# Where the low parts of some weights are made, and how far ahead branch B's operand is fetched, in a hybrid encoder layer

## The chip, the cores and the metric

The kernel runs on one core of a Trainium2 chip. The metric is device time in microseconds (us) for one execution, and the figure compared is the median of several runs. The engines are called by their names: TensorE (PE in the profile, its weight loads PEld) multiplies matrices, VectorE (DVE) and ScalarE (ACT) work elementwise, GpSimd (POOL) here only issues transfers, and SyncE (SP) issues nearly all other transfers. Every engine works through its own list of instructions in order. Sixteen DMA engines carry the transfers.

## The reference

One layer of an encoder with D = 1024, applied with the same weights to a prompt of 512 rows and a sample of 1024 rows, all in float32:

```
h = rms_norm(x, g_pre) * (1 + scale) + shift
p = h @ w_in                                   # 1024 x 8192
a_val, a_glu, a_z, u, v, b_z, g_a, g_b = split(p)
# branch A: convolution over time, 31 taps, per channel
hA = a_val * sigmoid(a_glu)
hA = silu(layer_norm(conv(hA) + conv_b)) * silu(a_z)
y_a = hA @ conv_proj
# branch B: gating over chunks of 128 rows
v  = layer_norm(gelu(v))
hB = gelu(u) * (w_s mixed over the rows of each chunk of v, + b_s) * silu(b_z)
y_b = hB @ sgu_proj
m  = sigmoid(g_a) * y_a + sigmoid(g_b) * y_b
out = x + gate * rms_norm(m @ w_out, g_post)
```

`shift`, `scale` and `gate` come from `silu(c) @ w_ada + b_ada`.

## The kernel before, in words

**Precision.** Each float32 operand X is split into a rounded high part Xh and a remainder Xl = X - Xh, and a product W X is three matmuls: Wh Xh, Wh Xl and Wl Xh. So every block of weights needs a high part `hi` and a low part `lo`, each 128x1024.

**A unit of weights.** One block of 512 KB is a `Unit`. `unit_load` has SyncE load it as `raw` (L222) four steps before its use; only four `raw` tiles exist, and four `hi` and four `lo`. `unit_act` runs about two and a half steps before the use: ScalarE casts `hi` from `raw` (L246). The low part is then made in one of two ways. With `by_dma` true, ScalarE writes -raw into `lo`, which rounds it to -hi (L249), and GpSimd issues a transfer that adds `raw` to it in place (L239, `lo<-raw` in the profile). With `by_dma` false, VectorE subtracts `hi` from `raw` (L258, `unit_dve`), and neither ScalarE's second pass nor the transfer is there.

**The steps.** TensorE's work is a list of steps, of 24 matmuls each where it multiplies by a block of weights (128x512 outputs, eight blocks of the contraction, three matmuls each):

| steps | work |
|---|---|
| 0 to 15 | prompt: convolution's value and gate columns |
| 16 to 23 | prompt: v (`steps_v`) |
| 24 to 79 | prompt: u, b_z, gates, a_z, the two projections (`col_step`) |
| 80 to 87 | prompt: w_out (`steps_o`) |
| 88 to 95, 96 to 103 | sample: v of half a, v of half b (`steps_v`) |
| 104 to 299 | sample: 28 pairs of column blocks, seven products each in place of eight (Strassen's way) |
| 300 to 315 | sample: branch B's projection of half a, then of half b (`post_B`) |
| 316 to 323, 324 to 331 | half a: branch A's projection (`post_A`), w_out |
| 332 to 339, 340 to 347 | half b: branch A's projection, w_out |

**What sets the order.** Python code writes the instructions out step by step: for each step it first emits the elementwise work that is due, then the matmuls, and then the loads that are due. Work that belongs to no step is a generator in the list `bg`; `fill` takes from it as long as a model clock of VectorE says that there is time. Small matmuls asked for by a generator are slipped into the middle of a step. `force` runs a generator to its end where a step needs its outcome. The model clock has constants written into the code, and no run goes back into it. So a line that is added for VectorE also moves where the generators' instructions stand on all engines.

**Around the sample's v.** While steps 88 to 103 run, a generator makes the operands of the pairs: sums and differences of halves of the sample (L928 to L936), with spills to and fetches from DRAM (`wk<-d`, L145). At the end of each half of v, VectorE takes the mean and variance (L544, L556), eight small matmul groups mix the rows of each chunk, and VectorE brings their outcomes out of PSUM (`mix_out`, L572). There are 8 PSUM banks in all.

**Around the end of the pairs.** The pairs spill hB, branch B's operand, to DRAM as eight blocks for each half. `hB_gen` fetches them again (L145), casts their high parts on ScalarE (L1266) and subtracts the low parts on VectorE (L1271). It runs for half a from step s_end - 6 = 294 and for half b from step 300, and fetches two blocks ahead. The convolution of the sample ends at about that place: its last outcome is stored to DRAM from `c` (L521, `d<-c`), and then `late_ln` fetches eight blocks of it (L145, `c<-d`) for its layer norm, which begins with small matmuls (L330, L331) on operands that ScalarE casts (L319). A little later the same pieces prepare branch A's operand (`hA`), whose low parts are written at L1231 and which half b needs from step 332.

Names in the profile: the matmuls of a column step are L448 to L450, of a step in `steps_v` or `steps_o` L471 to L473, and of the pairs L482 to L484; L1013 and L1125 are ScalarE's handling of the pairs' outcomes. Tiles: `wk` are 128x512 work tiles (11 buffers), `A` operand halves, `b` PSUM banks, `d` DRAM scratch.

Of the kernel before, what the change touches and what calls it, by code (L numbers as in the profile page):

```python
# [40 lines left out]
LAG = 1.0  # L41
PLAIN = 5.25
PROD = PLAIN / 2
LEAD_LOAD = 4 * PLAIN
LEAD_SPLIT = 2.4 * PLAIN

# [33 lines left out]
def layer_kernel(ctx: ExitStack, tc, x_p, x_s, xt_p, xt_a, xt_b, par, w_blk, w_v, cproj, sproj, w_out, w_ada, w_gate, wsT, bs,  # L80
# [121 lines left out]
    steps = []  # L202
# [167 lines left out]
    def start_bg(t, name, gen, first=False):  # L370
        setattr(t, name, gen)
        bg.insert(0, gen) if first else bg.append(gen)
# [118 lines left out]
        return st  # L491

    def col_step(t, src, act, a1=None, d1=None, d2=None, a2=None, pre=None, box=None, need=None, by_dma=True):
        u = Unit(src, len(steps), by_dma)

        def mm():
            b = bank()
            mm_cols(b, u, act())
            box[0] = b

        st = add_step(Step(mm, a1, d1, a2, d2, pre, need=need), u)

        def quarter(b, wh, wl, q):
            box[0] = b
            mm_quarter(b, wh, wl, act(), q)
        st.quarter = quarter
        return st
# [15 lines left out]
    def steps_v(t, need=None):  # L523

        for h in range(2):
            banks = []
            for kc in range(4):
                u = Unit(w_v[h, kc], len(steps))

                def mm(u=u, kc=kc, banks=banks):  # L530
                    if kc == 0:
                        banks[:] = [bank() for _ in range(4)]
                    mm_rows(banks, u, t.operand(), kc)

                def a1(h=h, banks=banks):
                    if h == 0:
                        t.v = t.v_home()
                        t.bn = smp.tile([P, 4, 12], F32, tag="bn", name="bn", bufs=1)
                    for i in range(4):
                        S.activation(t.v[:, i, h * T:(h + 1) * T], banks[i], AF.Gelu_apprx_tanh)  # L540

                def d1(h=h):
                    for i in range(4):
                        dv(0.65, lambda: V.bn_stats(out=t.bn[:, i, h * 6:h * 6 + 6], in_=t.v[:, i, h * T:(h + 1) * T]))  # L544

                def d2(h=h):
                    if h == 0:
                        return
                    mv = smp.tile([P, 4, 2], F32, tag="mv", name="mv")
                    for i in range(4):  # L550
                        dv(0.15, lambda: V.bn_aggr(out=mv[:, i, :], in_=t.bn[:, i, :].rearrange("p (c s) -> p c s", s=6)))
                    var = smp.tile([P, 4], F32, tag="ss", name="var")
                    dv(0.1, lambda: V.tensor_copy(var, mv[:, :, 1]))
                    r = rstd_small(var, 4, LN_EPS)
                    for i in range(4):
                        dv(0.65, lambda: V.tensor_scalar(t.v[:, i, :], t.v[:, i, :], mv[:, i, 0:1], r[:, i:i + 1],  # L556
                                                         op0=ALU.subtract, op1=ALU.mult))
                    if t.after_v:
                        t.after_v()
                last = kc == 3  # L560
                add_step(Step(mm, a1 if last else None, d1 if last else None, None, d2 if last else None,
                              act=2.2 if last else 0.0, need=need if h == 0 and kc == 0 else None), u)
# [20 lines left out]
    def steps_o(t, final, on_end=None):  # L583

        for h in range(2):
            banks = []
            for kc in range(4):
                u = Unit(w_out[h, kc], len(steps))

                def mm(u=u, h=h, kc=kc, banks=banks):  # L590
                    if kc == 0:
# [222 lines left out]
    sa, sb = Tile(), Tile()  # L814
# [177 lines left out]
    def pair(src1, src2, finish):  # L992
# [9 lines left out]
        def prod(name, wt, i, opn, first, last, a1=None, d1=None, a2=None, need=None, act=0.6):  # L1002
            def mm():
                if first:
                    st[name] = bank()
                mm_prod(st[name], half(w[wt][0], i), half(w[wt][1], i), A[opn], first, last)
            s_ = add_step(Step(mm, a1, d1, a2, dur=PROD, need=need, act=act))
            return s_
# [241 lines left out]
    def hB_gen(t):  # L1250
        xs = {}

        def fetch(j):
            if j < NK:
                x = wk()
                xs[j] = (x, load(x, outs["hB", t.half, j]))
        fetch(0)
        fetch(1)
        t.hB = new_act()
        kept = {}  # L1260
        for j in range(NK + 1):
            fetch(j + 2)
            if j < NK:
                x, tt = xs.pop(j)
                yield from until(tt)
                kept[j] = (x, ac(0.53, lambda: S.copy(t.hB.hi(j), x)))  # L1266
                yield "op"
            if j > 0:
                x, t1 = kept.pop(j - 1)
                yield from until(t1)  # L1270
                dv(0.62, lambda: V.tensor_sub(t.hB.lo(j - 1), x, t.hB.hi(j - 1).bitcast(F32)))  # L1271
                yield "op"
        t.hB_done = True
# [73 lines left out]
    def also(s, fn):  # L1347
        old = steps[s].extra

        def both():  # L1350
            if old:
                old()
            fn()
        steps[s].extra = both
# [17 lines left out]
        for j in range(0, NK, 2):  # L1372
            pair(w_blk[b0 + j], w_blk[b0 + j + 1], fin(j))
    s_end = len(steps)
    also(s_end - 6, lambda: start_bg(sa, "hBg", hB_gen(sa), first=True))
    post_B(sa)
    also(s_end, lambda: start_bg(sb, "hBg", hB_gen(sb), first=True))
    post_B(sb)
# [217 lines left out]
    for q in range(4):  # L1596
        for j in range(NH):
            u = q * NH + j
# [211 lines left out]
```

## Time and profile before

| | |
|---|---|
| runs | 1494.92, 1484.97 and 1494.02 us; median 1494.02 us |
| profiled execution | 1490.75 us, of which its span 1489.0 us |
| mean clock granted to TensorE | 0.986 of full speed |
| busy in the span | PE 1440.8 us (97%), PEld 1172.1 (79%), DVE 1089.2 (73%), ACT 776.4 (52%), POOL 216.9 (15%) |
| DMA | queue of SyncE 44.2% of 16 engines' span, queue of GpSimd 39.6% |

The busy time of an engine is the sum of its instructions' durations. In rows of windows the columns are the stretch, its length, then for each engine the busy time and, in brackets, the number of instructions, then the granted clock, the share of the DMA engines and what they moved. In rows of a timeline they are the start, the duration, the engine, the line, the operation and its tiles, the count, and in square brackets the idle time before the instruction with what ended it.

### The profile page before, as it was taken

To read this page: it belongs to the slowest core of one execution; us is meant where nothing else is said; L and a number is where in the kernel's file an instruction comes from. 1 tells how busy PE (TensorE), PEld (TensorE's weight loads), DVE (VectorE), ACT (ScalarE), POOL (GpSimd) and SP (SyncE) were. 2 spreads that over 40 slices of the span, in tenths; PEclk is the share of its full clock that TensorE was granted. 3 is DMA by queue.
4 is the path that set the end of the run, shared out by engine and by line. 5 is a ranking of instruction groups with operands and counts; after the bars stand their busy time and mean duration, and the time that the engine had idled before them with its cause. 6 is when DMAs were issued, how large, how long until landed. Compare 5 with 4: busy or idle time off the path is not lost.

```text
span 1489.0 us, 17873 instructions
## 1 busy us (share of the span) xinstructions
PE 1440.8 (97%) x6332; PEld 1172.1 (79%) x6332; DVE 1089.2 (73%) x1560; ACT 776.4 (52%) x1100; POOL 216.9 (15%) x256
## 2 busy tenths in 40 slices
PE   8999999999999998899999999999999969999997
PEld 4688888888888777788888888877878848888886
DVE  6769999985257344557999899889999847584424
ACT  4533545553685445454555565554556646556443
POOL 0001111111111111111111111111111101111110
PEclk9999999999999999999999999999999969999999
DMA  9268876998999999977666879987877799999994
GB/s 341 80 207 216 213 212 170 212 254 229 252 268 217 299 279 269 294 167 204 151 155 166 208 185 268 258 216 203 243 203 182 200 304 285 315 263 295 249 289 127
DMA packets 125225, 340.57 MB, mean 229 GB/s; under 512 B 13904, under 2 KB 17616, under 8 KB 124368
## 3 DMA queue, kind: packets, MB, share of 16 engines
q1 hardware_dynamic: 88992, 229.85, 44.2%
q0 software_dynamic: 36144, 109.59, 39.6%
q8 instruction: 49, 0.80, 0.2%
q14 instruction: 40, 0.33, 0.1%
HBM read 182.10 MB, written 47.71 MB: 154 GB/s over the span
## 4 chain that ended last, share of the span: by engine, by line
PE 68%; DMA 18%; DVE 7%; ACT 3%; issue 3%; SPq 2%; DVEq 0%; ACTq 0%; POOLq 0%
PE b L450 9%; PE b L449 9%; PE b L448 9%; PE b L482 9%; PE b L483 9%; PE b L484 9%; DMA raw<-in_w_blk_dram 4%; DMA raw<-in_w_v_dram 3%; DMA wk<-d 3%; PE b L471 3%; PE b L472 3%; PE b L473 3%; DMA c<-d 2%; DVE c L402 2%; DMA lo<-raw 1%
## 5 line engine op out<-in xcount | busy, mean ns | idle before, releaser
L448 PE MATMUL b<-A,hi 128*128 128x512 f32 x776 | 306.1, 394 | 10.7 <-ACT A L1266 10.7
L482 PE MATMUL b<-A,hi 128*128 128x512 f32 x784 | 306.3, 391 | 6.3 <-ACT wk L1013 6.3
L483 PE MATMUL b<-A,hi 128*128 128x512 f32 x784 | 305.2, 389 | 0.0
L484 PE MATMUL b<-A,lo 128*128 128x512 f32 x784 | 305.1, 389 | 0.0
L449 PE MATMUL b<-A,hi 128*128 128x512 f32 x776 | 305.1, 393 | 0.0
L450 PE MATMUL b<-A,lo 128*128 128x512 f32 x776 | 304.3, 392 | 0.3 <-DMA lo<-raw 0.2
L402 DVE SCALAR_TENSOR_TENSOR c<-c,prm 128x1024 f32<-128x1024 f32 x240 | 297.6, 1281 | 0.6
L246 ACT CAST hi<-raw 128x1024 fp32r<-128x1024 f32 x145 | 151.9, 1048 | 257.7 <-DMA raw<-in_w_v_dram 72.6
L239 POOL DMA_DIRECT2D lo<-raw x167 | 144.3, 864 | 797.0 <-ACT lo L249 695.3
L448 PEld LDWEIGHTS b<-A,hi 128*128 128x128 f32 x776 | 146.9, 189 | 43.8 <-ACT A L1266 13.3
L482 PEld LDWEIGHTS b<-A,hi 128*128 128x128 f32 x784 | 147.2, 188 | 39.4 <-ACT wk L1013 8.9
L449 PEld LDWEIGHTS b<-A,hi 128*128 128x128 f32 x776 | 146.8, 189 | 32.0 <-DVE A L1271 1.8
L450 PEld LDWEIGHTS b<-A,lo 128*128 128x128 f32 x776 | 147.0, 189 | 31.6 <-DMA lo<-raw 1.1
L484 PEld LDWEIGHTS b<-A,lo 128*128 128x128 f32 x784 | 147.2, 188 | 30.6
L483 PEld LDWEIGHTS b<-A,hi 128*128 128x128 f32 x784 | 147.2, 188 | 30.0
L402 DVE SCALAR_TENSOR_TENSOR S<-c,prm,S 128x512 f32<-128x512 f32 x240 | 162.5, 749 | 0.4
L472 PE MATMUL b<-lo,A 128*128 128x512 f32 x384 | 152.0, 396 | 9.1 <-DMA lo<-raw 9.1
L471 PE MATMUL b<-hi,A 128*128 128x512 f32 x384 | 152.3, 397 | 3.9 <-DVE wk L572 3.9
L473 PE MATMUL b<-hi,A 128*128 128x512 f32 x384 | 151.3, 394 | 0.0
L249 ACT ACTIVATE lo<-raw 128x1024 fp32r<-128x1024 f32 x139 | 146.7, 1056 | 0.0
L239 POOL DMA_DIRECT2D lo<-T x84 | 72.4, 862 | 448.0 <-ACT lo L1067 360.1
L1013 ACT COPY wk<-b 128x512 f32<-128x512 f32 x112 | 65.1, 586 | 119.8 <-PE b L484 116.1
(206 smaller groups left out, 1590.2 us busy)
## 6 DMA issues: line engine op xcount, KB each, us to landing
lo<-raw POOLq DMA_DIRECT2D x139, 512.0 KB, 6.9
raw<-in_w_blk_dram SPq DMA_DIRECT2D x105, 512.0 KB, 5.5
d<-wk SPq DMA_DIRECT2D x142, 256.0 KB, 3.9
wk<-d SPq DMA_DIRECT2D x116, 256.0 KB, 7.4
lo<-T POOLq DMA_DIRECT2D x28, 512.0 KB, 5.5
lo<-T POOLq DMA_DIRECT2D x56, 256.0 KB, 4.8
raw<-in_w_v_dram SPq DMA_DIRECT2D x24, 512.0 KB, 6.9
raw<-in_sproj_dram SPq DMA_DIRECT2D x24, 512.0 KB, 6.9
```

The costliest lines, as they stand in the source:

```text
L239: GP.dma_start(lo.bitcast(F32), src, accum_op=ALU.add)
L246: S.copy(u.hi, u.raw)
L402: lambda: V.scalar_tensor_tensor(acc, in0=win, scalar=wt, in1=acc, op0=ALU.mult, op1=ALU.add))
L448: PE.matmul(dst, lhsT=wh3[:, k, :], rhs=hi, start=(k == 0), stop=False)
L449: PE.matmul(dst, lhsT=wh3[:, k, :], rhs=lo, start=False, stop=False)
L450: PE.matmul(dst, lhsT=wl3[:, k, :], rhs=hi, start=False, stop=(k == NK - 1))
L471: PE.matmul(banks[i], lhsT=hi, rhs=wh3[:, kk, :], start=(k == 0), stop=False)
L472: PE.matmul(banks[i], lhsT=hi, rhs=wl3[:, kk, :], start=False, stop=False)
L473: PE.matmul(banks[i], lhsT=lo, rhs=wh3[:, kk, :], start=False, stop=(k == NK - 1))
L482: PE.matmul(dst, lhsT=wh3[:, k, :], rhs=hi, start=st, stop=False, skip_group_check=True)
L483: PE.matmul(dst, lhsT=wh3[:, k, :], rhs=lo, start=False, stop=False, skip_group_check=True)
L484: PE.matmul(dst, lhsT=wl3[:, k, :], rhs=hi, start=False, stop=sp, skip_group_check=True)
```

## The change

Three things are changed. First, in `steps_v` the units of odd steps get `by_dma` false, so that VectorE makes their low parts: 12 units, steps 17, 19, 21 and 23 of the prompt and 89 to 103 of the sample. Second, a constant `CONV_END = 88` makes the units of column steps and of w_out steps from step 88 on do the same at odd steps: 24 units in steps 300 to 347. Steps 24 to 87 stay with the transfer. Third, `hB_gen` fetches four blocks ahead in place of two, and for half a it is started at step 291 in place of 294; the operand's tile is still taken only from step 294 on (`hB_ok`).

```diff
+CONV_END = 88
 ...
     def col_step(t, src, act, a1=None, d1=None, d2=None, a2=None, pre=None, box=None, need=None, by_dma=True):
-        u = Unit(src, len(steps), by_dma)
+        u = Unit(src, len(steps), by_dma and (len(steps) < CONV_END or len(steps) % 2 == 0))
 ...
     def steps_v(t, need=None):
-                u = Unit(w_v[h, kc], len(steps))
+                u = Unit(w_v[h, kc], len(steps), len(steps) % 2 == 0)
 ...
     def steps_o(t, final, on_end=None):
-                u = Unit(w_out[h, kc], len(steps))
+                u = Unit(w_out[h, kc], len(steps), len(steps) < CONV_END or len(steps) % 2 == 0)
 ...
     def hB_gen(t):
-        fetch(0)
-        fetch(1)
+        for j in range(4):
+            fetch(j)
+        while not t.hB_ok():
+            yield "wait"
         t.hB = new_act()
         kept = {}
         for j in range(NK + 1):
-            fetch(j + 2)
+            fetch(j + 4)
 ...
-    also(s_end - 6, lambda: start_bg(sa, "hBg", hB_gen(sa), first=True))
+    also(s_end - 9, lambda: start_bg(sa, "hBg", hB_gen(sa), first=True))
+    free = set()
+    also(s_end - 6, lambda: free.add("hB"))
+    sa.hB_ok, sb.hB_ok = (lambda: "hB" in free), (lambda: True)
```

The lines of the changed program are numbered one higher from there on (L258 becomes L259, L572 becomes L573), and three higher after `hB_gen` (L1266 becomes L1269).

In the whole program 36 low parts go from the transfer to VectorE: its subtraction stands 42 times in place of 6, and ScalarE's pass for it and GpSimd's transfer 36 times less.

On SyncE, the first place is the end of the pairs, steps 295 to 301. Before, the fetches of hB's blocks 0, 1 and 2 (`d_7609`, `d_7705`, `d_7772`) stand ahead of the convolution's last store (from `c_5295`), and block 3 (`d_7868`) behind the eight fetches of `c`:

```order
L222 DMA raw<-in_sproj_dram 128x1024
L145 DMA wk<-d_7609 128x512
L145 DMA wk<-d_7705 128x512
L145 DMA wk<-d_7772 128x512
L521 DMA d_9333<-wk 128x512
L521 DMA d_9349<-c_5295 128x1024
L222 DMA raw<-in_sproj_dram 128x1024
L145 DMA c_9368<-d_6192 128x512
...
L145 DMA c_9368<-d_9349 128x512
L145 DMA wk<-d_7868 128x512
```

On SyncE after the change, at the same place, all eight blocks (`d_7597` to `d_8183`) stand ahead of the last store from `c_5283` and of the fetches of `c`:

```order
L146 DMA wk<-d_7597 128x512
L146 DMA wk<-d_7693 128x512
L146 DMA wk<-d_7760 128x512
L146 DMA wk<-d_7856 128x512
L522 DMA d_9242<-c_5283 128x1024
...
L146 DMA wk<-d_7923 128x512
L146 DMA wk<-d_8019 128x512
L522 DMA d_9329<-wk 128x512
L146 DMA wk<-d_8087 128x512
L146 DMA wk<-d_8183 128x512
L223 DMA raw<-in_sproj_dram 128x1024
L522 DMA d_9370<-c_5283 128x1024
```

So the five later blocks have moved past the store and past eight fetches. The load of `raw` behind them stays ahead of the store.

On VectorE, the second place is the middle of the sample's v, steps 97 to 100, where half a's mixes are brought out of PSUM. Before, the last two of the eight (L572) stand behind the four sums L933 to L936:

```order
L572 SCALAR_TENSOR_TENSOR wk<-b,prm,bias_t 128x512 x2
L928 TENSOR_TENSOR A<-wk,A 128x512
L930 SCALAR_TENSOR_TENSOR A<-wk,s_t,A 128x512
L572 SCALAR_TENSOR_TENSOR wk<-b,prm,bias_t 128x512 x2
L930 SCALAR_TENSOR_TENSOR A<-wk,s_t,A 128x512
L572 SCALAR_TENSOR_TENSOR wk<-b,prm,bias_t 128x512 x2
L933 TENSOR_TENSOR wk<-wk 128x512
...
L936 TENSOR_TENSOR wk<-wk 128x512
L572 SCALAR_TENSOR_TENSOR wk<-b,prm,bias_t 128x512 x2
L544 BN_STATS bn<-c_4833 128x6 x4
```

On VectorE after the change, at the same place, with the subtractions of the weights between (L259):

```order
L929 TENSOR_TENSOR A<-wk,A 128x512
L259 TENSOR_TENSOR lo<-raw,hi 128x1024
L573 SCALAR_TENSOR_TENSOR wk<-b,prm,bias_t 128x512 x2
L931 SCALAR_TENSOR_TENSOR A<-wk,s_t,A 128x512 x2
L573 SCALAR_TENSOR_TENSOR wk<-b,prm,bias_t 128x512 x6
L545 BN_STATS bn<-c_4816 128x6 x4
L259 TENSOR_TENSOR lo<-raw,hi 128x1024
L934 TENSOR_TENSOR wk<-wk 128x512
```

All eight mixes now stand ahead of that group of sums.

## The prediction

> **What bounds the kernel now.** The page comes first: which engine fills the span, and then what that engine waits for. TensorE is busy nearly all the time, so only its idle time and its half-clock time can be won back.
>
> ```profile
> PE 1440.8 (97%) x6332; PEld 1172.1 (79%) x6332; DVE 1089.2 (73%) x1560; ACT 776.4 (52%) x1100; POOL 216.9 (15%) x256
> ```
>
> The view of TensorE's waits (in total, times, longest) names three that matter:
>
> ```profile
> PE b L448 <- ACT A L1266: 10.7, 4, 8.3
> PE b L472 <- DMA lo<-raw: 9.1, 5, 2.9
> PE b L482 <- ACT wk L1013: 6.3, 5, 1.9
> ```
>
> The first is branch B's operand, the second low parts of weights that land late. Windows of 25 us and two long windows show where they lie:
>
> ```profile
> 500.00:525.00 25.00, 22.07 (x97) 17.96 (x97) 9.95 (x15) 12.10 (x20) 2.19 (x3) 1.00 1.00 291
> 525.00:550.00 25.00, 23.04 (x94) 18.57 (x94) 12.50 (x25) 14.26 (x21) 4.71 (x6) 0.93 0.99 263
> 575.00:600.00 25.00, 22.65 (x92) 18.29 (x93) 14.32 (x34) 11.25 (x17) 2.58 (x3) 0.93 0.97 265
> 625.00:650.00 25.00, 25.00 (x106) 20.55 (x105) 12.36 (x20) 13.60 (x22) 3.47 (x4) 0.94 0.92 257
> 1175.00:1200.00 25.00, 22.20 (x97) 17.63 (x95) 12.40 (x13) 11.30 (x18) 3.44 (x4) 1.00 1.02 287
> 1200.00:1225.00 25.00, 15.06 (x28) 8.61 (x29) 10.87 (x18) 11.35 (x17) 1.72 (x2) 0.52 0.94 302
> ```
>
> ```profile
> 516.38:646.54 130.16, 117.15 (x522) 95.82 (x520) 64.57 (x114) 63.80 (x91) 17.24 (x20) 0.96 0.97 275
> 1225.00:1475.00 250.00, 249.78 (x1100) 206.11 (x1099) 133.26 (x227) 137.91 (x189) 37.89 (x44) 1.00 0.97 270
> ```
>
> The last window is TensorE without loss: 249.78 / 1100 = 0.227 us a matmul, although the DMA engines are busy to 0.97 there. From 1175 to 1225 only 97 + 28 = 125 matmuls run, worth 125 x 0.227 = 28.4 us, so **place B, the end of the pairs, loses 50 - 28.4 = 21.6 us**. **Place A, from the prompt's w_out through the sample's v** (516 to 647), has 130.16 - 117.15 = 13.0 us idle. It loses a little more to the clock: three windows were granted 0.93, 0.93 and 0.94 in place of 1.00, so 25 x 0.07 = 1.75, 1.75 and 25 x 0.06 = 1.5 us. TensorE's own timeline names A's waits:
>
> ```profile
> 519.70 0.50 PE L472 MATMUL b<-lo,A 128*128 128x512 f32 x1 [2.93 <-DMA lo<-raw]
> 538.27 0.50 PE L472 MATMUL b<-lo,A 128*128 128x512 f32 x1 [1.96 <-DMA lo<-raw]
> 576.17 0.50 PE L472 MATMUL b<-lo,A 128*128 128x512 f32 x1 [2.45 <-DMA lo<-raw]
> 590.11 0.50 PE L472 MATMUL b<-lo,A 128*128 128x512 f32 x1 [1.18 <-DMA lo<-raw]
> 624.43 0.80 PE L471 MATMUL b<-hi,A 128*128 128x512 f32 x1 [3.93 <-DVE wk L572]
> ```
>
> By the order of steps these are w_out's step 85, and of the sample's v the steps 88, 94, 96 and 100. The clock follows three of them (538, 576, 624) and not the longest `lo` wait at 519.70, whose window has 1.00. The Trainium skill, "TensorE: Matmul & The Clock Gate", section "Why this matters for your kernels", asks that idle gaps stay under about 3 us, since one idle window gives half the clock; the trace disagrees in part, with waits of 1.96 and 2.45 us ahead of a reduced clock. By that rule a wait under 3 us costs no clock, so 1.75 us less would be won at 576 and the forecast would be 1470.
>
> **Part 1: low parts by VectorE.** One exchange has these prices:
>
> ```profile
> L258 DVE TENSOR_TENSOR lo<-raw,hi 128x1024 fp32r<-128x1024 f32 x6 | 7.3, 1224 | 9.7 <-ACT hi L246 9.6
> L249 ACT ACTIVATE lo<-raw 128x1024 fp32r<-128x1024 f32 x139 | 146.7, 1056 | 0.0
> lo<-raw POOLq DMA_DIRECT2D x139, 512.0 KB, 6.9
> q0 software_dynamic: 36144, 109.59, 39.6%
> ```
>
> VectorE gains 36 x 1.224 = 44.1 us of work, ScalarE loses 36 x 1.056 = 38.0 us, and on the way of one weight 1.056 us of ScalarE, about 0.9 us of GpSimd's issue and 6.9 us of transfer give way to 1.224 us. In the DMA engines one such transfer takes 0.524 / 109.59 of 39.6% of 1489 us, 2.82 us; 36 of them free 101 us of DMA time.
>
> At A, VectorE has 64.57 of 130.16 us busy, and the 8 subtractions there, 9.8 us, find room. In the prompt, 4 x 1.224 = 4.9 us fall where VectorE is full, but they only delay the convolution's taps behind them, and later it stands mostly idle:
>
> ```profile
> 150.00:175.00 25.00, 24.95 (x110) 20.33 (x110) 25.00 (x39) 15.41 (x20) 4.30 (x5) 1.00 1.01 251
> 375.00:400.00 25.00, 24.90 (x110) 20.20 (x109) 4.76 (x7) 13.62 (x20) 4.29 (x5) 1.00 0.96 231
> ```
>
> 25 - 4.76 = 20.2 us are free in that one window: price nothing. Without that cover, it would be 4.9 us.
>
> Now A's waits one by one. Steps 85 and 88: their transfers and all ahead of them are the same after the change, since step 85 keeps the transfer and 88 is even. Their 2.93 and 1.96 us, and 1.75 us of clock behind the second, stay. Step 94: it is even and keeps its transfer, but those of steps 91 and 93, ahead of it in the queue, are gone, 2 x 2.82 = 5.6 us of transfer against a wait of 2.45: it goes, with its 1.75 us of clock, 4.2 us. Step 100: TensorE waits for a PSUM bank which the last two L572 free, and in the order these now stand ahead of the sums that held them:
>
> ```profile
> 576.07 0.69 DVE L936 TENSOR_TENSOR wk<-wk 128x512 f32<-128x512 f32 x1 [1.56 <-DMA wk<-d]
> 620.62 0.69 DVE L933 TENSOR_TENSOR wk<-wk 128x512 f32<-128x512 f32 x1 [7.75 <-DMA wk<-d]
> ```
>
> L933 sat 7.75 us until its fetch landed. With the L572 ahead of it the 3.93 us and 1.5 us of clock go, 5.4 us. Step 93 (the rest of the 13.0, 0.6 us) goes with its transfer. Together 4.2 + 5.4 + 0.6 = 10.2 us. Step 96 is the one that can give some back. Its chain runs through the fetch for L936 above, a spill behind it on SyncE, and only then the loads:
>
> ```profile
> 577.22 0.93 SPq L222 DMA_DIRECT2D raw<-in_w_v_dram  x2
> 584.86 0.86 POOL L239 DMA_DIRECT2D lo<-raw  x1 [11.12 <-PE b L473]
> ```
>
> The low part issued at 584.86 landed when TensorE's wait ended at 590.11. Nothing in this chain gets earlier by the change except the contention, while TensorE arrives 4.8 us sooner (step 93 and 94). So between 0 and 4.8 + 1.18 = 6 us are waited here, before 1.18; I take 3.4 (the freed 2.82 of one transfer taken off 6, and a little back for a queue that stays busy), which is 2.2 more than before. **A gives 10.2 - 2.2 = 8 us**; bounds 0 (fetches for the sums remain late and all moves along) and 11.4 (10.2 and the 1.18).
>
> **Part 2: late steps by VectorE, 300 to 347.** TensorE has no idle time there to win after 1225, so the exchange is worth nothing by itself. What could be lost: VectorE works in order, and a subtraction whose `hi` is late holds it. It has 133.26 of 250 us busy, and 23 of the 24 new ones add 28.2: room is there.
>
> **Part 3: hB's blocks, four ahead.** The chain of waits through place B, SyncE's queue and the two ends:
>
> ```profile
> 1186.20 7.17 DMA d<-c
> 1193.77 4.79 DMA c<-d
> 1198.57 6.83 DMA wk<-d
> ```
>
> ```profile
> 1191.51 0.58 ACT L1013 COPY wk<-b 128x512 f32<-128x512 f32 x1
> 1204.78 1.27 ACT L1266 CAST A<-wk 128x512 fp32r<-128x512 f32 x2 [11.30 <-DMA wk<-d]
> ```
>
> ```profile
> 1201.93 0.33 SPq L222 DMA_DIRECT2D raw<-in_sproj_dram  x1
> raw<-in_sproj_dram SPq DMA_DIRECT2D x24, 512.0 KB, 6.9
> ```
>
> SyncE waits 7.17 us for the convolution's store, issues the fetches of `c` while the first of them takes 4.79, and only then reaches block 3, which needs 6.83 more; ScalarE's cast sits 11.30 us for it and TensorE 8.25 (the 8.3 above). In the order after, every fetch of hB stands ahead of store and `c`. From 1186.20 a block would land within 6.83, at 1193; ScalarE casts in about 0.64 (1.27 for two). TensorE came to that block at 1204.78 + 0.64 - 8.3 = 1197.1, and to the operand some 2 us sooner: the wait goes.
>
> What is late next, since the weights of steps 303 to 305 are loaded behind the same eight fetches? The `raw` of L222 at 1201.93 stands behind them before; the store and the eight fetches still stand ahead of it, three fetches of hB no longer do, but a spill of ScalarE's late outcomes does, so I leave it at about 1203. Then 6.9 for landing, 1.05 and 1.06 for ScalarE's two passes, 0.9 for the issue and 6.9 for the low part: 1203 + 16.8 = 1219.8, which by the order is step 304's, an even step. TensorE without a wait is there four steps of 24 x 0.227 = 5.45 us after about 1196, at 1217.7: 2.1 us late. With the contention of eight 512 KB fetches, up to 6. The casts of hB also stand between ScalarE's snapshots of the last pair (L1013), which can hold step 299 by 0.5 to 2.8 us; this comes ahead of the same late weight and so is not added. I take 3.5 us, nearest to the row of the landing. **B gives 21.6 - 3.5 = 18 us**, bounds 21.6 - 8.6 = 13 and 20.8 (a cast late by 0.8).
>
> The Trainium skill, "DMA: Bandwidth & Descriptors", section "Anatomy of one DMA — SWDGE (gpsimd) path", fits 2.0 us and bytes / 436e3 to such a transfer: 3.2 us as an estimate for 512 KB. The trace's median is 6.9, more than double, with the engines busy to 0.97; by the page step 304's weight would be there 3.7 us sooner and the time 2 to 4 us lower.
>
> **The sum.** 1490.75 (the profiled execution) - 8 - 18 = 1464.75. The median of the runs stands 1494.02 - 1490.75 = 3.3 above the profiled one, so 1468.
>
> **The rivals.**
> *R1, A's chain only moves.* For it: the fetch for L936 and the one of 7.75 us are on no path that the change shortens. Then A gives 0 to 2, and 1490.75 - 1 - 18 + 3.3 = 1475.
> *R2, the late weights take B's place.* Against the 2.1 us above stands that SyncE waits for the store with the load behind it, and that block fetches and `c` fetches now run together. If the load of 304 goes out and lands as late as a second such chain (4.79 + 6.83 more), 10 to 14 us of B come back: 1468 + 12 = 1480.
> *R4, the change does not do what it says.* The blocks are fetched sooner but the operand's tile is taken at step 294 as before; if the casts or subtractions stand behind something else until 1205, B gives 0 to 4: 1490.75 - 8 - 2 + 3.3 = 1484.
> *R3, slower.* VectorE's line is in order, and in steps 300 to 331 stand 16 new subtractions, each behind a `hi`. The last low part of hA for half b was written here, well ahead of its use at step 332:
>
> ```profile
> 1377.51 1.46 DVE L1231 TENSOR_TENSOR A<-wk,A 128x512 fp32r<-128x512 f32 x2
> 1393.08 0.39 PE L448 MATMUL b<-A,hi 128*128 128x512 f32 x1
> ```
>
> The slack is 1393.08 - 1378.97 = 14.1 us. In the order after, that work stands two steps later, 10.9 us, which leaves 3.2. If each subtraction holds VectorE for its `hi`, 16 holds beyond 3.2 us delay TensorE one for one, and the gain of 26 is gone at (26 + 3.2) / 16 = 1.8 us each. At 3 us, 48 - 3.2 = 45 us are lost: 1468 + 45 = 1513. Against it: the six subtractions of before sat 9.7 us in all, 1.6 each, but early, with loads just begun; and from 1225 on the loads keep up.
>
> **How the numbers follow.** Forecast 0.57 (1461 to 1475), R1 0.17 (1472 to 1478), R2 0.13 (1477 to 1485), R3 0.07, R4 0.06. The range takes the forecast's lower bounds, A at 11.4 and B at 20.8 without the 3.3 of the median, which is 1458.6, and some spread of the runs, whose lowest is 5.8 below the profiled one: 1453. Above it reaches over R1 and most of R2: 1482. A change of 1% is 14.9 us, about what a measurement of this kernel can tell from none; the bound is at 1479. Faster: 0.57 + 0.17 and a third of R2, 0.78; same: the rest of R2 and 0.05 of R4, with a small part of R3, 0.15; slower 0.07.
>
> **What would show it.** TensorE's waits: L448 for the cast of hB's blocks at most 2 us in place of 10.7; no wait of step 100 for L573; waits for `lo<-raw` of about 2.9 and 2.0 still there at steps 85 and 88, and 2 to 5 us at 96; in steps 303 to 305 one wait of 2 to 6 us for `lo<-raw` or `hi`. Window 1225 to 1475 still at 0.227 us a matmul. Wrong it is if step 304 waits over 8 us, if a wait for L1231's successor stands at step 332, or if the sample's v keeps 11 us or more of idle time.

## The result, and the profile after

The changed kernel takes 1470.14 us (median of four runs, 1466.83 to 1472.45) against 1491.85 us before (four runs, 1484.97 to 1494.92). The ratio is 0.986, with a 95% interval from 0.982 to 0.990. It was forecast at 1468 us, with a range of 1453 to 1482. The profiled execution took 1466.83 us, of which its span is 1464.9 us, 24.1 less than before. By the medians the gain is 21.7 us, and 18.8 us (1490.13 to 1471.35) in a later comparison of the same two kernels.

The page of the kernel after and its view of TensorE's waits (total, times, longest):

```profile
PE 1432.5 (98%) x6332; PEld 1169.3 (80%) x6332; DVE 1129.0 (77%) x1596; ACT 742.3 (51%) x1064; POOL 186.2 (13%) x220
```

```profile
PE b L483 <- ACT wk L1014: 6.9, 6, 2.1
PE b L473 <- DMA lo<-raw: 5.0, 4, 2.6
PE b L331 <- ACT wk L320: 4.1, 2, 2.6
```

VectorE gained 39.8 us of work and ScalarE lost 34.1, near the 44.1 and 38.0 of the prediction. The wait for hB's casts (10.7 us before) has left the list, and so has the one for L572. A new name has come in: L331, the small matmul of `late_ln`'s mean, which waits for ScalarE's cast of its operand.

The windows of the kernel after that answer to those shown of before:

```profile
500.00:525.00 25.00, 22.09 (x90) 17.47 (x89) 9.83 (x14) 11.94 (x20) 1.73 (x3) 0.93 1.00 281
525.00:550.00 25.00, 23.33 (x103) 18.96 (x102) 15.29 (x27) 12.50 (x20) 3.43 (x4) 1.00 0.91 260
550.00:575.00 25.00, 25.00 (x112) 20.70 (x111) 13.65 (x19) 9.91 (x13) 0.86 (x1) 1.00 0.85 264
575.00:600.00 25.00, 24.56 (x117) 20.33 (x116) 19.35 (x40) 14.62 (x20) 2.60 (x3) 1.00 0.80 260
1175.00:1200.00 25.00, 23.82 (x98) 19.56 (x99) 6.21 (x9) 8.91 (x16) 1.26 (x2) 0.93 0.93 280
1200.00:1225.00 25.00, 22.23 (x97) 17.75 (x96) 21.92 (x34) 15.76 (x23) 1.72 (x2) 1.00 0.96 323
```

From 550 on, the sample's v now runs nearly without idle time, with the DMA engines at 0.85 and 0.80 where they stood at 0.99 and 0.97. From 1175 to 1225, 98 + 97 matmuls run where there were 125 (step 300 begins 8.9 us earlier here than before); but some time is still lost.

TensorE's own timeline, put together by steps (from a step's first matmul to the next one's; a full step is 5.44 us, a product of the pairs 2.72), says where the 24.1 us come from:

| stretch | before, us | after, us | gain, us |
|---|---|---|---|
| start to step 85 | 516.38 | 517.45 | -1.1 |
| A: steps 85 to 103 | 130.16 | 117.77 | 12.4 |
| the pairs, steps 104 to 289 | 520.93 | 519.63 | 1.3 |
| the last ten products, 290 to 299 | 27.53 | 31.22 | -3.7 |
| B: steps 300 to 302 | 38.51 | 16.32 | 22.2 |
| B: steps 303 to 307 | 27.71 | 35.43 | -7.7 |
| step 308 to the end | 227.78 | 227.08 | 0.7 |

The last ten products and B together gain 10.8. The rows behind the two losses, from TensorE's, ScalarE's and VectorE's timelines of the kernel after (start, duration, instruction, idle time before it):

```profile
1176.18 0.61 PE L483 MATMUL b<-A,hi 128*128 128x512 f32 x1 [2.13 <-ACT wk L1014]
1207.82 0.50 PE L331 MATMUL b<-wk,onemr 128*128 128x512 f32 x1 [2.55 <-ACT wk L320]
1229.70 0.50 PE L331 MATMUL b<-wk,onemr 128*128 128x512 f32 x1 [1.52 <-ACT wk L320]
```

```profile
1172.09 1.05 ACT L247 CAST hi<-raw 128x1024 fp32r<-128x1024 f32 x1 [3.45 <-DMA raw<-in_sproj_dram]
1174.53 1.12 ACT L1269 CAST A<-wk 128x512 fp32r<-128x512 f32 x2
1175.55 1.06 ACT L1014 COPY wk<-b 128x512 f32<-128x512 f32 x2
1199.84 1.05 ACT L247 CAST hi<-raw 128x1024 fp32r<-128x1024 f32 x1 [12.49 <-DMA raw<-in_sproj_dram]
1207.15 0.62 ACT L320 CAST wk<-wk 128x512 fp32r<-128x512 f32 x1 [2.57 <-issue]
```

```profile
1200.92 1.22 DVE L259 TENSOR_TENSOR lo<-raw,hi 128x1024 fp32r<-128x1024 f32 x1 [15.26 <-ACT hi L247]
1203.27 0.68 DVE L1292 TENSOR_TENSOR S<-b,wk 128x512 f32<-128x512 f32 x1
1203.87 2.48 DVE L421 TENSOR_TENSOR wk<-wk,c 128x512 f32<-128x512 f32 x4
1206.38 0.69 DVE L423 TENSOR_TENSOR wk<-wk 128x512 f32<-128x512 f32 x1
```

At 1176, TensorE waits 2.13 us for ScalarE's copy of a pair's outcome out of PSUM (L1014), called a snapshot below. The snapshot stands behind two casts of hB (L1269) and, ahead of these, behind the casts of a weight (L247) whose `raw` lands late: counted from the start of step 290 these casts begin 17.2 us in (1172.09 - 1154.85), and in the kernel before 15.8 us in (1183.23 - 1167.47):

```profile
1183.23 1.06 ACT L246 CAST hi<-raw 128x1024 fp32r<-128x1024 f32 x1 [3.06 <-DMA raw<-in_sproj_dram]
```

At 1207 TensorE waits in the middle of step 303 for the mean's operand, which comes from a row of sums on VectorE that ends with L421 and L423. VectorE sat 15.26 us ahead of the subtraction of step 303's weight, with the sums behind it. That hold is not what made them late, though: ahead of L421 stands also L1292, branch B's own work, which needs a block fetched from DRAM, and by the trace this fetch, issued at 1196.87, landed only at 1203.03. Without the subtraction L1292 could have begun at 1203.03 in place of 1203.27, and the mean would have come some 0.2 us sooner.

### The profile page after: what moved, and what is told of

Its sections match the earlier page's. It is cut to its first block, busy times and chain, and to the rows that moved or that the text cites. A ratio compares the mean times of both kernels' runs of the same rounds, so it can differ in the third digit from the quotient of the medians.

```text
span 1464.9 us, 17769 instructions
## 1 busy us (share of the span) xinstructions
PE 1432.5 (98%) x6332; PEld 1169.3 (80%) x6332; DVE 1129.0 (77%) x1596; ACT 742.3 (51%) x1064; POOL 186.2 (13%) x220
## 4 chain that ended last, share of the span: by engine, by line
PE 80%; DMA 11%; DVE 4%; issue 2%; ACT 2%; SPq 1%; DVEq 0%; ACTq 0%; POOLq 0%
PE b L451 11%; PE b L449 11%; PE b L450 11%; PE b L483 10%; PE b L484 10%; PE b L485 10%; PE b L473 4%; PE b L474 4%; PE b L472 4%; DMA lo<-raw 2%; DMA wk<-d 2%; PE b L568 1%; DMA raw<-in_w_blk_dram 1%; DMA raw<-in_sproj_dram 1%; DVE c L403 1%
## 5 line engine op out<-in xcount | busy, mean ns | idle before, releaser
L247 ACT CAST hi<-raw 128x1024 fp32r<-128x1024 f32 x145 | 152.0, 1048 | 262.4 <-DMA raw<-in_w_v_dram 61.7
L240 POOL DMA_DIRECT2D lo<-raw x131 | 113.4, 865 | 788.8 <-ACT lo L250 690.8
L449 PEld LDWEIGHTS b<-A,hi 128*128 128x128 f32 x776 | 146.1, 188 | 30.4 <-issue 0.2
L1014 ACT COPY wk<-b 128x512 f32<-128x512 f32 x112 | 65.0, 585 | 121.2 <-PE b L485 117.5
L250 ACT ACTIVATE lo<-raw 128x1024 fp32r<-128x1024 f32 x103 | 108.7, 1055 | 0.0
```

The costliest lines, as they stand in the source:

```text
L240: GP.dma_start(lo.bitcast(F32), src, accum_op=ALU.add)
L247: S.copy(u.hi, u.raw)
L449: PE.matmul(dst, lhsT=wh3[:, k, :], rhs=hi, start=(k == 0), stop=False)
```

## The experiments

All kernels were timed against the kernel before on the same chip; the ratio is to it, with its 95% interval. "The first edit" is v's weights, "the second" the late steps 300 to 347, "the third" hB's fetches.

| run | ratio | interval | A, us | steps 290 to 299 | B, us |
|---|---|---|---|---|---|
| first edit alone | 0.9961 | 0.9939 to 0.9982 | 120.6 | 27.4 | 64.7 |
| third edit alone | 0.9990 | 0.9965 to 1.0014 | 127.8 | 30.3 | 58.0 |
| second edit alone | 1.0004 | 0.9979 to 1.0029 | 128.3 | 27.3 | 64.4 |
| first and third | 0.9940 | 0.9919 to 0.9961 | 119.5 | 30.4 | 55.5 |
| first and third, mean put back | 0.9896 | 0.9875 to 0.9918 | 119.3 | 32.1 | 53.7 |
| the kernel after, again | 0.9872 | 0.9845 to 0.9900 | 117.3 | 32.2 | 49.9 |
| after, mean put back | 0.9863 | 0.9842 to 0.9885 | 119.7 | 31.7 | 47.5 |
| after, start at 294 | 0.9930 | 0.9911 to 0.9946 | 120.1 | 27.4 | 62.3 |
| after, w_out too | 0.9871 | 0.9838 to 0.9903 | 116.5 | 31.6 | 50.2 |
| after, all waits at once | 0.9900 | 0.9871 to 0.9930 | 118.2 | 31.4 | 50.4 |
| the same, casts later | 0.9946 | 0.9929 to 0.9964 | 118.3 | 29.4 | 58.8 |
| after, traffic put back | 0.9881 | 0.9851 to 0.9911 | 123.4 | 31.4 | 49.5 |

A and B are steps 85 to 103 and 300 to 307 of one profiled execution each; the ratios rest on four to ten runs.

### The three edits apart

The first edit alone:

```diff
-                u = Unit(w_v[h, kc], len(steps))
+                u = Unit(w_v[h, kc], len(steps), len(steps) % 2 == 0)
```

> The kernel before with the first edit alone (odd steps of the sample's and the prompt's v by VectorE). Theory: all that stretch A (start of step 85 to start of step 104) gained belongs to this edit, so it takes about 118 us in place of 130.2, and place B (start of step 300 to start of step 308) stays at about 66 us; the profiled execution is then about 1479 us. Rival: the gain in A is only kept because the later edits keep DMA traffic low, or is given back in the pairs, whose stretch of 548.5 us would grow by most of the 12; then 1486 to 1490.

Measured: 1483.66 us against 1488.34, a gain of 4.7 us by the medians. A took 120.6 us, close to the theory, and B stayed at 64.7. The pairs before step 290 grew by 2.5 us (523.48), much less than A won, and the same stretch takes 519.4 to 528.1 us over the twelve runs of the table, none of which has an edit in that stretch. So the gain in A belongs to this edit. The profiled execution itself, 1488.33 us, lies where the rival put it; but it came to step 85 4.4 us later than the kernel before, and 2.7 of these had been lost by step 16, ahead of the first edited weight. By the medians the gain is smaller than in A.

The third edit alone (the start at s_end - 9, four fetches ahead, the operand's tile at s_end - 6):

> The kernel before with the third edit alone (hB's blocks four ahead, from step 291). Theory: it carries most of what B gained, but with every late low part by transfer the weight of step 303 has its raw at about 1200 and its low part some 10 us later, 6 to 7 us after TensorE wants it; B takes 54 to 57 us in place of 66.2, the wait for the mean's cast (L320 in the kernel after) is gone, and the profiled time is 1480 to 1485. Rival: the late edit is worth nothing at B, then B takes 51.8 as in the kernel after, with the same waits for the mean, and the time is about 1479.

Measured: 1485.74 us, a ratio of 0.999, not told apart from no change. Both theories missed B, which took 58.0 us, and the first theory's wait for a late weight isn't there. TensorE's waits in this kernel:

```profile
PE b L482 <- ACT wk L1013: 13.3, 7, 4.6
PE b L330 <- ACT wk L319: 10.7, 2, 10.0
```

The wait for hB's block is gone, but the mean's matmul (L330) waits 10.05 us in step 301, which takes 16.97 us. By the order this matmul stands behind 48 matmuls of branch B here, and behind 24 in the kernel before. There TensorE stood waiting for hB until the mean's operand was nearly there, and waited 2.0 us for it:

```profile
1219.01 0.80 PE L330 MATMUL b<-wk,onemr 128*128 128x512 f32 x1 [2.02 <-ACT wk L319]
```

One wait has taken much of the place of the other: steps 300 to 302 take 30.3 us, against 38.5 before and 16.3 in the kernel after, which waits for nothing there.

The second edit alone (odd steps from 300 on by VectorE):

> The kernel before with the second edit alone (odd steps of 300 to 347 by VectorE). Theory: nothing to win, since TensorE has no idle time after 1225 us and the wait for hB's block at step 300 does not hang on it: A 130, B 64 to 66, the time within 3 us of 1490.8. Rival: the subtractions hold VectorE at B or in steps 316 to 331; then B grows, or step 332 starts late by more than 3 us, and the time is over 1495.

Measured: 1488.28 us, ratio 1.0004. That is what the theory said: nothing by itself.

The first and third together:

> The kernel after without the second edit (late steps by transfer). Theory: A as in the kernel after, about 118 us; B 54 to 57 in place of 51.8, because the weight of step 303 then waits for a transfer in place of a subtraction; the profiled time is 1469 to 1472 against 1466.8. Rival one: the same as the kernel after, within 1 us, since the edit was worth nothing. Rival two: faster, since VectorE is no longer held 15 us ahead of the sums for the mean: B under 50, time about 1463.

Measured: 1479.56 us, ratio 0.994. The time was missed by 8 us on the slow side. Again it is the mean, as TensorE's waits show:

```profile
PE b L330 <- ACT wk L319: 10.1, 2, 8.1
PE b L482 <- ACT wk L1013: 8.4, 6, 2.9
PE b L472 <- DMA lo<-raw: 6.1, 4, 2.7
```

Here too it stands behind 48 matmuls. The second edit, worth nothing alone, takes the ratio from 0.994 to 0.987 where the other two are made. In the kernel after, its subtractions move the model clock of VectorE on, and with it the place where the mean is asked for: behind 84 matmuls, in the middle of step 303. The operand itself isn't sooner: it is ready 1209.2 - 1190.0 = 19.2 us after the start of step 300 without the second edit, and 1207.8 - 1186.1 = 21.7 us after it with the edit. Without the subtraction ahead of the sums, VectorE is held by branch B's L1291 (L1292 in the kernel after) and its fetch, and the last sum, L422, stands behind it:

```profile
1207.16 0.69 DVE L1291 TENSOR_TENSOR S<-b,wk 128x512 f32<-128x512 f32 x1 [4.39 <-DMA wk<-d]
1207.77 0.68 DVE L422 TENSOR_TENSOR wk<-wk 128x512 f32<-128x512 f32 x1
```

Not all of the second edit's worth lies at B. This profile also waits 1.98 us for the mean of half b, at step 315, and from step 308 to the end it takes 232.2 us, against 227.1 in the kernel after:

```profile
1291.15 0.50 PE L330 MATMUL b<-wk,onemr 128*128 128x512 f32 x1 [1.98 <-ACT wk L319]
```

### The mean's place

If that is right, the kernel of the first and third edits must gain when only the mean is put back, and the weight of step 303 must then be late, since it comes by transfer there.

```diff
-        box = pe_later(LAG, 0.43, go)
+        box = pe_later(lag, 0.43, go)
 ...
-        yield from ln_gen(t, t.acc)
+        yield from ln_gen(t, t.acc, 8.0 if t is sa else LAG)
```

> The first and third edits without the late low parts by VectorE, but with late_ln's mean of half a asked for 7 us later by the model clock, so that it stands behind 84 matmuls of branch B as in the kernel after (behind 48 without that). Theory one: the late edit's whole worth is that it pushed the mean back; then the wait of 8.1 us is gone, B is 50 to 52 us as in the kernel after, and the time within 2 us of it. Theory two: the late edit also shortens the way of step 303's weight, by transfer about 10 us longer; then step 303 waits 4 to 7 us for lo<-raw, B is 53 to 57 us and the time 3 to 6 us above the kernel after.

Measured: 1475.17 us against 1471.35 for the kernel after in the same comparison, 3.8 more. The mean's wait is gone, and the weight's has come, in step 303, as theory two had it:

```profile
1211.01 0.79 PE L450 MATMUL b<-A,lo 128*128 128x512 f32 x1 [6.91 <-DMA lo<-raw]
```

So the second edit does two things at B: it moves the mean (ratio 0.9940 to 0.9896, measured in two comparisons), and it shortens the way of step 303's weight (0.9896 to 0.9872, whose intervals overlap; the row above shows the wait). The first of these is not B's alone: with the mean put back, the stretch from step 308 on falls from 232.2 to 228.2 us as well. Whether a kernel with the second and third edits and without the first behaves in the same way wasn't tried.

The kernel after was timed again beside it:

> The kernel after, unchanged, timed again beside the kernels of this call, so that they are compared on one chip. All theories: 0.98 to 0.99 of the kernel before; place B (start of step 300 to start of step 308) 51 to 53 us, the first mean of late_ln waiting 2 to 3 us in step 303.

Measured: 1471.35 against 1490.13 us, ratio 0.9872; B 49.9 us, with a wait of 2.2 us for the mean.

What the kernel after itself still loses to the mean, by asking for it 3 us later (the same diff on the kernel after, with 4.0 in place of 8.0):

> The kernel after, but in late_ln of half a the two small mean matmuls are asked for 3 us later by the model clock, so that they stand behind 96 and 192 matmuls of branch B in place of 84 and 168. Theory: what is left at B is TensorE waiting at the head of its line for the mean's cast (2.55 and 1.52 us, with 3 to 5 us of half clock and the matmuls themselves); then step 303 falls from 9.3 to under 6 us, steps 306 and 307 from 15.3 to under 12.5, B to 44 to 47 us, and the time is 5 to 7 us below the kernel after. Rival, as the prediction had it: the weights of steps 303 to 305 are late; then the wait shows as one for lo<-raw or for the subtraction and B stays at 50 or more.

Measured: 1469.76 us, 1.6 less than the kernel after, which the intervals don't tell apart. Step 303 fell from 10.1 to 5.9 us, the theory's sign, and then the rival's came one step later:

```profile
1217.91 0.50 PE L451 MATMUL b<-A,lo 128*128 128x512 f32 x1 [2.46 <-DMA lo<-raw]
```

This is step 304, an even one, whose weight comes by transfer: the prediction's 2.1 us, hidden until now behind the mean. Step 304 took 8.25 us, 2.8 more than a full step, of which the wait is 2.46. Of 4.2 us won, 2.8 were given back.

### Depth or start

```diff
-    also(s_end - 9, lambda: start_bg(sa, "hBg", hB_gen(sa), first=True))
+    also(s_end - 6, lambda: start_bg(sa, "hBg", hB_gen(sa), first=True))
```

> The kernel after, with four blocks ahead but the generator of half a started at step 294 as before. By the order, blocks 0 to 4 then stand ahead of the convolution's last store and of the fetches of c, blocks 5 to 7 behind them, and the first mean stands behind 24 matmuls of branch B. Theory: the start at 291 is what clears the queue; here TensorE still waits at step 300, for block 5, and steps 300 to 302 take 28 to 36 us in place of 16.3, B 58 to 65 us, the time 8 to 13 us above the kernel after. Rival: depth is enough, B stays under 54 us.

Measured: 1478.97 us, 7.6 above the kernel after; B 62.3 us, steps 300 to 302 34.6 us. TensorE's timeline shows the wait for the sixth block, which stands behind the store and the fetches of `c` again:

```profile
1200.28 0.80 PE L449 MATMUL b<-A,hi 128*128 128x512 f32 x1 [7.24 <-ACT A L1269]
1207.02 0.80 PE L450 MATMUL b<-A,hi 128*128 128x512 f32 x1 [3.02 <-DVE A L1274]
```

Four blocks ahead are not enough; the three steps of earlier start clear SyncE's queue. The last ten products, on the other hand, take 27.4 us here as before: the early start is what costs the 4 us there. A start at step 291 with two blocks ahead wasn't tried, so how much the depth adds to the start stays open.

### What is left in A

Prompt's w_out at odd steps by VectorE as well, on the kernel after:

```diff
-                u = Unit(w_out[h, kc], len(steps), len(steps) < CONV_END or len(steps) % 2 == 0)
+                u = Unit(w_out[h, kc], len(steps), len(steps) % 2 == 0)
```

> The kernel after, with the prompt's w_out too (odd steps 81, 83, 85, 87) by VectorE. Theory: the waits left in A hang on the transfers of steps 85 and 87 as the prediction had it; step 85 falls from 9.9 to 5.4 us, step 88 from 7.4 to 5.4 or a little over, A from 117.5 to 110 to 113, and the time is 5 to 8 us below the kernel after (about 1464 where that takes 1471). Rival: the loads of raw, not the low parts, are late there; then the same wait stands at L472 or for hi and A stays over 116.

Measured: 1470.61 us, a ratio of 0.9871 to the kernel before, as the kernel after has (0.9872). Step 85 did fall to 5.4 us, but step 88 rose to 11.0:

```profile
538.23 0.55 PE L473 MATMUL b<-lo,A 128*128 128x512 f32 x1 [3.68 <-DMA lo<-raw]
```

TensorE came to step 88 at 534.16, 4.1 us earlier than in the first profile of the kernel after, and the low part of step 88, issued at 527.78, took 10.4 us to land at 538.2, with the DMA engines busy all the time (1.02 in the window from 527 to 539). The wait moved on; of the 4.5 us won at step 85, 3.6 were lost at 88. A came out over 116 us, as the rival had it, but the wait is for a low part and not for `raw`.

To see whether the shorter way or the smaller traffic helped in v, traffic was put back, two stores to DRAM for each addition in SBUF that had gone, with the order on the other engines unchanged:

```diff
             dv(1.14, lambda: V.tensor_sub(w, r, h.bitcast(F32)))
+            if 88 <= u.first < 104:
+                for _ in range(2):
+                    GP.dma_start(scratch(D), r)
```

> The kernel after with two transfers of 512 KB from each raw of steps 89 to 103 at odd steps to DRAM scratch, which nobody reads: the traffic of the low parts is put back, while the way of each weight and the order on the other engines stay as in the kernel after. Theory: step 96's wait was short because with less traffic the fetches of the sample's sums landed sooner (its chain moved up by 4 us); with the traffic back they land late again, steps 93 to 97 take 25 to 29 us in place of 22.5, A rises to 121 to 126, the time by 4 to 8 us. Rival: the shorter way of the odd weights is all; A stays within 2 us of 117.5.

Measured: A rose to 123.4 us, and the place is step 94, not 96:

```profile
578.00 0.80 PE L476 MATMUL b<-lo,A 128*128 128x512 f32 x1 [4.78 <-DMA lo<-raw]
617.66 3.43 DVE L576 SCALAR_TENSOR_TENSOR wk<-b,prm,bias_t 128x512 f32<-128x512 f32 x4 [2.87 <-PE b L571]
```

```profile
550.00:575.00 25.00, 23.22 (x103) 18.91 (x101) 11.92 (x15) 10.38 (x14) 3.92 (x6) 1.00 0.98 337
575.00:600.00 25.00, 22.00 (x86) 17.85 (x87) 18.23 (x40) 11.81 (x18) 2.81 (x4) 0.86 0.99 309
```

With the transfers back, the DMA engines are at 0.98 and 0.99 again, and step 94 waits again. That agrees with the traffic as the cause of that step's gain, but it doesn't show it: in the profile of the second edit alone, which keeps every transfer of the kernel before in v, step 94 has no wait either (5.44 us, where the other two profiles without the first edit have 9.77 and 8.33). Steps 96 and 100 stay short with the traffic (5.6 and 5.5 us). For step 100 this settles the cause. The four fetches that the sums wait for land at 618.1 to 621.1 us by this trace, about as step 100 begins (620.05), and so did those of the kernel before (619.9 to 622.9, step 100 at 618.98). Yet the last mixes, which now stand ahead of the sums (L576 here, the second row above), wait for TensorE's own small matmuls and for no fetch, and step 100 doesn't wait. So it is the order that frees it. The median, 1471.01 us, however, is not above that of the kernel after (1471.35), though the two were timed in different comparisons; how much of the 6 us reaches the end stays open.

### All remaining waits at once

The kernel after with w_out at odd steps and step 304 by VectorE and the mean 3 us later:

> The kernel after with the prompt's w_out at odd steps and step 304 by VectorE, and half a's means of late_ln asked for 3 us later (by the order behind 108 and 216 matmuls of branch B). Theory: the waits of 2 to 3 us left at steps 85, 88, 303 and 304 all go; A 110 to 113, B 44 to 46 (floor 8 x 5.44 = 43.5 and the mean matmuls), the time 8 to 13 us below the kernel after, 1459 to 1463. Rival: step 304's subtraction holds VectorE ahead of other work, and what is won there is lost at steps 305 to 308 (B over 48).

Measured: 1473.95 us, 3.3 above the kernel with w_out alone in the same comparison, though their intervals overlap. B took 50.4 us: VectorE's extra subtraction now stands among the sums for the mean, and step 304 takes 11.8 us with waits for L320 and L321, the mean's high and low part. And at step 332 there is a wait that no kernel above has:

```profile
1379.15 0.50 PE L450 MATMUL b<-A,hi 128*128 128x512 f32 x1 [4.08 <-DVE A L1232]
```

That is half b's hA, the place of the prediction's slower rival. The same with the operand of half a taken two steps later, and its means asked for another 8 us later by the model clock:

> As the kernel with all these edits, but half a's operand is taken two steps later (step 296), so that by the order one snapshot of the last pair stands ahead of the first casts of hB on ScalarE, and the means stand behind 84 and 216 matmuls. Theory: the 4 us at steps 296 and 297 come from the two casts (1.1 us) and from weights that load later behind four fetches of hB (1.5 us); without the casts PE waits there under 1 us, steps 296 and 297 take 5.5 to 7 us in place of 9.5, and up to 4 us more are won, if the casts that now come later do not hold step 300. Rival: hB's casts then come late and step 300 waits for them; the time is above the kernel with all edits.

Measured: 1480.58 us. Steps 296 and 297 fell to 7.7 us, 1.3 less than in the kernel with all edits, from which it differs in the casts and the means. So the casts ahead of the snapshot are only a part of that loss. Here none stands ahead of it, and TensorE still waits 1.91 us: ScalarE sat 5.32 us for a `raw` that lands late, as in the kernel after:

```profile
1174.43 1.05 ACT L247 CAST hi<-raw 128x1024 fp32r<-128x1024 f32 x1 [5.32 <-DMA raw<-in_sproj_dram]
1177.47 0.50 PE L483 MATMUL b<-A,hi 128*128 128x512 f32 x1 [1.91 <-ACT wk L1014]
```

Step 300 now waits for the casts and subtractions that come late:

```profile
1195.25 0.79 PE L449 MATMUL b<-A,hi 128*128 128x512 f32 x1 [5.22 <-ACT A L1269]
1202.63 0.79 PE L450 MATMUL b<-A,hi 128*128 128x512 f32 x1 [6.59 <-DVE A L1274]
```

No kernel tried is clearly faster than the kernel after.

## Why the prediction was right, and where it wasn't

The time was right: 1470.1 against 1468. The terms were not, and that the time came out so near is in part luck. The gain was forecast at 26 us; the spans of the two profiled executions give 24.1, the medians 21.7 and, timed again, 18.8. And the forecast started from 1494.02 us, 3.3 above the profiled execution, where the later medians of the kernel before are 1488.3 to 1491.9: a start too high and a gain too large came out near the time measured.

**A, 8 us with bounds 0 and 11.4.** This trace has 12.4. Over the seven profiles that have the first edit and nothing else changed in A, it takes 117.3 to 120.6 us, 119.2 in the mean, and over the three without it 127.8 to 130.2, 128.7 in the mean; so 9.5 is the better figure, and the one trace was a good one. Steps 85 and 88 kept their waits (2.61 and 1.67 us). Step 100 lost its own by the order of the mixes, as worked out: it takes 5.5 us in all seven and 10.1 to 11.9 in the three, 5.5 us of the 9.5. Step 94 was put at 4.2 us; it takes 5.4 to 5.9 us in the seven and 7.85 in the mean of the three, 2.3 us, since one of the three doesn't wait there.

Step 96 was mis-sized, put at 3.4 us of wait: it is 0.44 in this trace and at most 2.32 in the seven, against 1.18 to 1.86 in the three. "Nothing in this chain gets earlier by the change except the contention" is contradicted here: the sum L937 ran at 572.1 in place of 576.07, and the loads behind it went out at 573.2 in place of 577.2. That less traffic made them earlier is not shown: in the profile of the second edit alone, with all transfers in place, the same sum ran at 572.8, and step 96 waited 1.74 us. The prompt's four subtractions cost little, as forecast: steps 16 to 79 take 360.9 to 362.4 us in the seven and 360.4 to 361.1 in the three.

**B, 18 us with bounds 13 and 20.8.** Measured 10.8 with the last ten products (11.7 in the kernel's second profile), outside the bounds, whose 8.6 us are not derived there. What came back, 21.6 - 10.8 = 10.8 us, is the size of rival R2 (10 to 14 us), by another cause than R2's late weight; it was the better A and the high start that kept the time near 1468. Step 300's wait went as forecast. What took its place was named wrongly. The prediction had the weight of step 304; the traces have, first, the late snapshot, behind hB's casts and a late `raw`, 3.7 us over the last ten products, which had been seen as "0.5 to 2.8 us" and was left out of the sum because it was thought to lie ahead of the same wait; and second, the mean of `late_ln`, with 3.8 us in step 303 and 4.4 in 306 and 307. The prediction never looked at that matmul, though in the list of TensorE it stands inside branch B, and a wait of 2.0 us for it can be read in the trace before. The late weight of 304 is real and is 2.46 us, but it shows only when the mean is out of its way.

**Part 2 at nothing.** True alone (ratio 1.0004) and wrong in the sum: with the other two edits it takes the ratio from 0.994 to 0.987. The 18 us were booked to the third edit alone, which gives 0.999 alone. The step that failed is "worth nothing by itself" as an argument about the three together: it looked at what VectorE and the transfers do after 1225, and not at where the edit puts other instructions, nor at step 303, where the subtraction was done at 1202.1 and a transfer would have landed at 1211.0 (its row is in the experiment with the mean put back, in which step 300 began 1.1 us later).

**The slower rival.** Of the new subtractions one found its `hi` very late, by 15.26 us, at step 303; no other held VectorE for more than 1.3 us before step 332 began. The long hold cost the mean next to nothing, since work that stood behind it needed a fetch that landed at 1203.03 (see the rows behind the two losses, above). At step 332 the slack was worked out as 3.2 us; in the profile after it is 2.0:

```profile
1366.71 0.69 DVE L1232 TENSOR_TENSOR A<-wk,A 128x512 fp32r<-128x512 f32 x1 [2.07 <-ACT A L1241]
1369.40 0.39 PE L449 MATMUL b<-A,hi 128*128 128x512 f32 x1
```

The last low part ends at 1367.40, and step 332 begins at 1369.40. In the kernel that went for all waits at once, with one more subtraction and later means at B, it was used up.

**After 1225.** The window of the kernel after from 1240 on is still without loss, 200.00 / 884 = 0.226 us a matmul, with less traffic than before:

```profile
1240.00:1440.00 200.00, 200.00 (x884) 165.57 (x883) 125.69 (x186) 98.86 (x137) 15.56 (x18) 1.00 0.78 234
```

## What to carry to other kernels

When a wait on an engine that works in order is taken away, go through what stands next in that engine's own list, small matmuls of other work included, and ask of each when its operand is ready; here, with the earlier fetches alone, the mean's matmul, 48 matmuls into branch B, took back 14.0 of the 22.2 us that steps 300 to 302 had to win. Where a model clock places background work, an edit that does nothing on the hardware at its own place can still decide by where it moves that work, so edits must be priced together and in the order that comes out. A total that fits is no proof of its terms: in the profile of the kernel after, A came out 4.4 us better than forecast and B 7.2 worse, which the table by steps shows. And a long idle time ahead of an instruction is no proof that it delays what stands behind it: look at what that would have waited for next.

## What the hardware showed that was not expected

TensorE's clock does not follow the length of a wait. At step 85 a wait of 2.93 us before the change cost the step 8.67 - 5.44 = 3.2 us, little more than itself, and one of 2.61 us after it cost 9.94 - 5.44 = 4.5 us; its window was granted 1.00 in the first case and 0.93 in the second. In the repeated profile 2.30 us cost 4.2, and at step 88 a wait of 1.67 us cost 2.0. The Trainium skill, "TensorE: Matmul & The Clock Gate", section "Why this matters for your kernels", puts the limit at idle gaps of about 3 us; these runs have half clock after 2.30 and 2.61 us and none after 2.93, so here a wait of 2 to 3 us may or may not cost some 1.9 us more. One such case is more than half of the 3.2 us by which the seven profiles with the first edit differ in A.
